# One run of up to 16 KB per partition instead of rows of 4 KB: the weight loads of a three-layer block on one Trainium2 core

## The chip, the cores and the metric

The kernel runs on one core of one Trainium2 chip. The metric is the time on the device of one execution, in microseconds; three runs of the kernel before are given. A profile is one more execution, recorded by the hardware profiler, with its own span. Rates are in GB/s of 10^9 bytes; a load of 2 MB means 2 x 1024 x 1024 bytes, which is 16 KB for each of the 128 partitions of the on-chip memory.

## What is computed

All in float32, on 256 tokens of 1024 features. First a block with attention in three branches (compressed, selected, window) beside a short convolution, and then a mixture of 64 experts, two of which serve each token:

```python
h = rms_norm(x, norm1_w) * (1 + sc1) + sh1
proj = h @ w_in
mix = rms_norm(concat(nsa_attention(...), short_conv(...)))
x = x + g1 * (mix @ w_out)
h2 = rms_norm(x, norm2_w) * (1 + sc2) + sh2
x = x + g2 * hier_moe(h2, ...)   # sum over a token's experts: weight * ((silu(h2 @ w1[e]) * (h2 @ w3[e])) @ w2[e])
```

Then two more layers: one mixes with a Fourier transform and a window attention that also sees 256 context tokens, the other with pooling; each is followed by a gated FFN of 2816 hidden features, `(silu(h @ w1) * (h @ w3)) @ w2`, and a last norm closes the whole. The shifts, scales and gates (`sh`, `sc`, `g`) of every layer are `silu(c) @ ada_w + ada_b`, 6 x 1024 columns a layer.

Of the weights the experts are the bulk: w1, w3 and w2 of 64 experts are 64 x 3 x 2 MB = 402.7 MB of the 589.5 MB that the DMA engines move.

## The kernel before

The host lays the inputs out (`_pack_inputs`) and the kernel computes. Nearly all weights pass through one ring of six buffers (`RING = 6`), the tiles named `w` of 128 partitions x 4096 floats, 16 KB a partition, 2 MB each. `wslot` takes the next buffer and issues one load from SyncE (SP), at L438 in the profile; the load waits until the engines have read what was in that buffer six loads ago. SP issues the loads in the order in which the program asks for them, on one queue that 16 DMA engines serve together. The program's order on the other engines is fixed at build time; a small model of the time (`_Model`, `weave`) orders the work of the front and of the second block, and its times for the loads are counted from the bytes of a slot.

The stages are, in order: the front (modulation, projections, attention, routing of the first block), the experts, the second block's Fourier and attention layer (`even`), its FFN, the pooling layer, and the last FFN. The expert stage runs over 16 quads of four experts. A quad gathers up to 32 tokens for each of its experts (tiles `xg`), multiplies them by w1 and w3 (`quad_h`, output `ps<-w,xg`), gates (`g`, `gT`), multiplies by w2 (`ps<-w,gT`), and adds the weighted results to `x`. `load_experts` brings each of the three weights of a quad in four loads; a load holds, for every partition, a part of the rows of all four experts, cut at L1435:

```python
src = self.a[n][4 * q:4 * q + 4].rearrange("e (p c k) f -> p c e (k f)", c=4, k=m)
```

So a partition of a slot is filled from four places in DRAM, one per expert, 2 MB apart, each a row of 4 KB. Twelve such loads make a quad. The first quad's third weight part that does not fit the ring (`EXTRA`) goes to four small tiles `piece`, and the last load of the stage is made as two halves of 1 MB with rows of 2 KB.

Before quad 8 stands a loop for experts with more than 32 tokens (`overflow`, its branch at L1523). It runs zero times on this input, but its branch is a meeting of all engines, and SP's part in it waits for the landing of all loads that SP has issued.

Other weights come as follows: the modulation weights (`w_ada`, `ada_w_2`, function `ada_rows`) in rows of 4 KB, four to a partition, their first two loads in rows of 2 KB; the projections (`win`, `wout`, `win2`, `wout2`) in rows of 4 KB per tile of 128 columns, the first in halves of 2 KB; the first weights of the compression (`cw1`) in rows of 1 KB; the second FFN weight (`f2`) in rows of 4 KB. The first FFN weight (`f13`) has already one run of 16 KB per partition.

Of the kernel before, what the change touches and what calls it, by code (L numbers as in the profile page):

```python
# [16 lines left out]
P = 128  # L17
# [27 lines left out]
# ------------------------------------------------------------------ layouts  # L45
# [158 lines left out]

def _pack_inputs(x):
# [6 lines left out]
    w = x["w_in"][0][:, _win_cols()].reshape(KT, P, 20, P)  # L212
    ins["win"] = np.ascontiguousarray(w.transpose(2, 1, 0, 3))
    ins["wval"] = x["w_in"][0][:, _val_cols()].reshape(KT, P, 280).transpose(1, 0, 2)
    w = x["w_out"][0][_mix_perm()].reshape(KT, P, KT, P)
    ins["wout"] = np.ascontiguousarray(w.transpose(2, 1, 0, 3))
    ins["w_ada"] = x["w_ada"][0]
# [6 lines left out]
    w = x["mix_in_w_2"][0][:, tiles].reshape(KT, P, 10, P)  # L224
    ins["win2"] = w.transpose(2, 1, 0, 3)
    rows = np.concatenate([np.arange(512), 512 + _mix_perm()[:512]])
    w = x["mix_out_w_2"][0][rows].reshape(KT, P, KT, P)
    ins["wout2"] = w.transpose(2, 1, 0, 3)
# [3 lines left out]
    ins["f2"] = x["ffn_w2_2"].reshape(2, NC, 2, P, D)  # L232
# [24 lines left out]
class _Model:  # L257
    """estimates when the engines are done with what has been issued so far"""
# [27 lines left out]
    def ready(self, *aps, engine="tensor", write=False):  # L286
        """when an engine can read (or write) them"""
# [8 lines left out]
    def last(self, name):  # L296
        """the last access of a tile so far"""
# [35 lines left out]
class _Net:  # L333
# [19 lines left out]
    # ---- small helpers  # L353
# [9 lines left out]
    def room(self, tag, n=1):  # L363
        """when the next n banks are free, for weave"""
# [5 lines left out]
    def grab(self, tag="g", n=1):  # L370
        """the next n banks, kept until release()"""
# [54 lines left out]
    def wslot(self, src, load=None):  # L426
        """next slot of the weight ring, filled from src ([128, ...] in DRAM)"""
        t = self.ring.tile([P, 4096], F32, tag="w", name=self.nm("w"))
        shape = src.shape
        n = int(np.prod(shape[1:]))  # L430
        dst = t[:, :n]
        if len(shape) == 3:
            dst = dst.rearrange("p (a b) -> p a b", a=shape[1])
        elif len(shape) == 4:
            dst = dst.rearrange("p (a b c) -> p a b c", a=shape[1], b=shape[2])
        self.slots_us.append(self.more_us + n * 512 / 360e3)
        self.more_us = 0.0
        d = self.nc.sync.dma_start(dst if load is None else dst[:, :, load], src if load is None else src[:, :, load])  # L438
        self.loads.append(d)
# [6 lines left out]
    def at(x, k):  # L446
        """feature tile k of x, a tile [128, 8, n] or a list of its feature tiles"""
# [28 lines left out]
    def loaded(self, n):  # L476
        """when slot n of the ring has arrived, for weave"""
# [12 lines left out]
    def front_slots(self, name, srcs, load=None):  # L490
        """slots of the ring ahead of their use: number and tile"""
        for src in srcs:
            self.ahead.setdefault(name, []).append((len(self.slots_us), self.wslot(src, load)))
# [12 lines left out]
    def event(self, name, *aps):  # L506
        """when an event has come and these are ready, for weave"""
        return lambda: self.ready(*aps) if name in self.events else math.inf

    # ---- setup  # L510
    def setup(self):
# [8 lines left out]
        # the scale of half the features, and the weight that meets them  # L520
        win0 = self.front_src("win0")
        for h in range(2):
            self.front_slots("ada1", [a["w_ada"][:, D + 512 * h:D + 512 * h + 512].rearrange("(k p) f -> p k f", p=P)])
            half = slice(512 * h, 512 * h + 512)
            if h == 0:
                self.front_slots("win0", [win0], load=half)
            else:
                nc.sync.dma_start(self.ahead["win0"][0][1][:, :, half], win0[:, :, half])
# [7 lines left out]
        # silu of the conditions  # L536
# [44 lines left out]
    def ada_cols(self, slots, h, st, bias, out):  # L581
        """512 columns of the same, in one slot"""
# [23 lines left out]
    def ada2(self, i):  # L606
        """part i of the modulation of layer 0, for the tokens and the context"""
# [3 lines left out]
    def gemv0(self, i):  # L611
        o = slice(8 * i, 8 * i + 8)
        yield from self.gemv(None, 0, self.sil[:, :8], self.vec("b_ada")[:, o], self.mod0[:, o], f"ada{i}")
        self.events[f"ada{i}"] = self.ready(self.mod0[:, o])

    def gemv(self, w, col0, c, bias=None, out=None, slots=None):
        """1024 columns of cond @ w + bias as a column tile [128, 8], on the vector engine; in steps.
        Without out, the sum over the partitions and the bias are left for later"""
        nc = self.nc
        acc = self.ph(D, "acc")  # L620
        for h in range(2):
            if slots:
                t = yield from self.take(slots, h)
            else:
                t = self.wslot(w[512 * h:512 * h + 512, col0:col0 + D].rearrange("(k p) f -> p k f", p=P))
# [31 lines left out]
    def gemv2(self, layer, i):  # L657
        o = 48 * layer + 8 * i
        return self.gemv(self.a["ada_w_2"][layer], D * i, self.sil[:, 8:16], self.vec("ada_b_2")[:, o:o + 8],
                         self.mod2[:, o:o + 8])  # L660
# [10 lines left out]
    def squares(self, x):  # L671
        """sum over the feature tiles of x * x"""
# [8 lines left out]
    def norm(self, x, acc=None):  # L681
        """1 / rms of the tokens of x [128, 8, 256] (feature major), on every partition; acc: its squares, summed"""
# [12 lines left out]
    def scaled(self, w, scale):  # L695
        """w * (1 + scale) per feature"""
# [4 lines left out]
    def norm_mod(self, x, s, shift, out=None, parts=None, acc=None):  # L701
        """x / rms * s + shift per feature, to out or as two float32r parts"""
# [27 lines left out]
    def bias_table(self):  # L730
        """T[p, h, j] = bias of head h at distance p + 128 - j"""
# [14 lines left out]
    def headnorm(self, src, w, outs, newton=False, tag="n"):  # L746
        """src [128, n] over the rms of its 64 row groups, times w; outs: (rows, tile) pairs"""
# [18 lines left out]
    def front_src(self, n):  # L766
# [3 lines left out]
        if n == "kv":  # L770
            return a["win2"][0:2].rearrange("t p k f -> p t (k f)")
        c = int(n[-1])
        if n[:-1] == "conv":
            return a["win"][8 + 3 * c:11 + 3 * c].rearrange("t p k f -> p t (k f)")
        if n[:-1] in ("win", "wout"):
            return a[n[:-1]][4 * c:4 * c + 4].rearrange("t p k f -> p t (k f)")
        return a["cw1"][c].rearrange("(j p) f -> p j f", p=P)

    def front_loads(self):
        a = self.a  # L780
        for n in ORDER:
# [5 lines left out]
            if n[:3] == "ada":  # L787
                w = a["ada_w_2"][0] if len(n) > 4 else a["w_ada"]
# [5 lines left out]
            self.front_slots(n, srcs)  # L794

    def proj(self):
        """the input projection of the tiles that run ahead of the shift of the modulation"""
# [5 lines left out]
        self.kz = self.ph(0, "kz", shape=[P, 2, S])  # rows (group, feature); branch, key  # L803
# [10 lines left out]
        self.wint = [self.ahead[f"win{c}"][0][1][:, i, :] for c in range(2) for i in range(4)]  # L814
# [10 lines left out]
        def tiles():  # L825
            for c in range(2):
# [3 lines left out]
                for k in range(KT):  # L830
# [4 lines left out]
                    for i in range(4):  # L835
                        self.mm(ps[i][:, :S], lhsT=self.wint[4 * c + i][:, P * k:P * k + P], rhs=h[:, k, :],
# [11 lines left out]
    def share(self):  # L848
        """the shift: its share in the tiles that ran ahead of it, and h; then the blocks to compress"""
# [6 lines left out]
        for c in range(2):  # L856
# [3 lines left out]
            for k in range(KT):  # L860
                j = k % 4
                self.mm(ps[32 * j:32 * j + 32, :], lhsT=sh[:, k, :], rhs=t0[:, :, P * k:P * k + P], start=k < 4, stop=k > 3,
                        tile_position=(0, 32 * j))
# [23 lines left out]
        # (v g0, v g1, k g0, k g1), half, block, pair  # L887
        A = self.A = self.ph(0, "A", shape=[P, 4, S]).rearrange("p c (i b j) -> p c i b j", i=2, j=8)
        for c in range(4):
# [5 lines left out]
            for i, rows in enumerate((LOW, HIGH)):  # L895
                # token 16 b + 2 j (+ 1 in the upper rows), j within the half
# [6 lines left out]
    def qk(self, i):  # L903
        """a tile of q (i < 4), k_slc or k_win"""
# [6 lines left out]
    def values(self):  # L911
        """v_slc, v_win and the gates: token major"""
# [17 lines left out]
    def hidden(self):  # L930
        """hidden layer of the compression"""
# [1096 lines left out]
```

## Time and profile before

| | us |
|---|---|
| median of 3 runs | 1760.09 (1758.51 to 1763.04) |
| span of the profiled execution | 1758.2 |
| of it: PE (matrix multiplies) busy | 1349.1 |
| VectorE (DVE) busy | 575.0 |
| ScalarE (ACT) busy | 375.8 |
| GpSimd (POOL) busy | 143.2 |
| data moved by DMA | 589.5 MB, mean 335 GB/s |

The page of a profile cuts the span into 40 slices of 44 us and gives for each the busy tenths of every engine, of the 16 DMA engines, and the GB/s moved. Its chain of waits follows the work that ended last back to what released it. A window is a stretch of the span in us from its start. The DMA view of a window counts packets, by sizes, and the bytes that began in it; a packet is one run of contiguous bytes to one partition on one DMA engine, and a few packets of 4 bytes are the signals that a load has landed. Time to landing is counted from the issue of a load to the arrival of its last byte, time in the queue included.

### The profile page before, as it was taken

What the parts mean: (1) busy time and instruction counts of PE and PEld (TensorE: products, weight loads), DVE (VectorE), ACT (ScalarE), POOL (GpSimd) and SP (SyncE); (2) the same over time, 40 slices, a digit from 0 to 9 for tenths busy, and PEclk for the clock granted to TensorE, in tenths of its full rate; (3) what the DMA queues carried; (4) which work ended last, traced back from release to release, by engine and by line L of the source; (5) the groups of instructions that cost most, each with busy time, mean ns of one, the idle gap of its engine ahead of it and who ended that gap; (6) DMA issues with size and microseconds to landing.
All of it is one profiled execution on the core that took longest, in us unless ns stands there. A gap on an engine that the chain in (4) does not pass through costs nothing.

```text
span 1758.2 us, 18422 instructions
## 1 busy us (share of the span) xinstructions
PE 1349.1 (77%) x7664; PEld 782.4 (45%) x7664; DVE 575.0 (33%) x1109; ACT 375.8 (21%) x704; POOL 143.2 (8%) x80
## 2 busy tenths in 40 slices
PE   7999976665675665566667566658998999999997
PEld 5676832221221221221122122215676787778886
DVE  1567711110110111011011011103766787554443
ACT  2345210000000000100000000003324444544444
POOL 0000000000000000000000000000201323212224
PEclk9999988888887888688888788889998999999999
DMA  9787999999999999899999999999476787635610
GB/s 380 252 335 300 343 361 408 409 409 409 409 409 409 409 409 409 323 409 409 409 409 408 409 409 409 409 409 388 166 266 251 276 335 300 260 144 191 264 72 24
DMA packets 144811, 589.51 MB, mean 335 GB/s; under 512 B 4840, under 2 KB 9064, under 8 KB 141136
## 3 DMA queue, kind: packets, MB, share of 16 engines
q1 hardware_dynamic: 143584, 584.82, 84.7%
q0 software_dynamic: 704, 2.64, 0.4%
q8 instruction: 63, 1.03, 0.2%
q10 hardware_dynamic: 432, 0.79, 0.1%
q14 instruction: 28, 0.23, 0.0%
HBM read 587.16 MB, written 1.06 MB: 335 GB/s over the span
## 4 chain that ended last, share of the span: by engine, by line
PE 33%; DMA 22%; DVE 3%; ACT 1%; issue 0%; DVEq 0%; ACTq 0%
PE ps L250 33%; DMA w<-in_w 21%; DVE acc L250 1%; DMA w<-in_ada_w 0%; DVE wlo L250 0%; DVE p L250 0%; ACT p L250 0%; DVE x L250 0%; ACT rstd L250 0%; DVE ada L250 0%; DVE sqa L250 0%; DVE mix L250 0%; ACT mix L250 0%; ACT sq L250 0%; DVE nt L250 0%
## 5 line engine op out<-in xcount | busy, mean ns | idle before, releaser
L250 PE MATMUL ps<-w,xg 128*32 128x512 f32 x2032 | 303.5, 734 | 210.1 <-DMA w<-in_w 210.1
L250 PE MATMUL ps<-w,gT 128*32 128x512 f32 x1024 | 177.6, 830 | 120.1 <-DMA w<-in_w 113.5
L250 PEld LDWEIGHTS ps<-w,xg 128*32 128x32 f32 x2032 | 65.2, 125 | 430.9 <-DMA w<-in_w 218.9
L250 ACT ACTIVATE whi<-w 128x1024 fp32r<-128x1024 f32 x132 | 139.4, 1059 | 151.4 <-PE ps L250 145.8
L250 DVE TENSOR_TENSOR g<-g,ps 128x512 f32<-128x512 f32 x16 | 11.0, 688 | 482.5 <-PE ps L250 482.5
L250 DVE TENSOR_TENSOR wlo<-w,whi 128x1024 fp32r<-128x1024 f32 x88 | 114.7, 1311 | 111.5 <-ACT whi L250 111.4
L250 PEld LDWEIGHTS ps<-w,gT 128*32 128x32 f32 x1024 | 33.7, 136 | 247.4 <-DMA w<-in_w 163.5
L250 PE MATMUL ps<-whi,mix 128*128 128x512 f32 x352 | 140.0, 403 | 4.1 <-ACT mix L250 4.1
L250 DVE SCALAR_TENSOR_TENSOR acc<-w,sil,acc 128x1024 f32<-128x1024 f32 x98 | 141.8, 1447 | 2.3 <-DMA w<-in_ada_w 0.8
L250 POOL TENSOR_TENSOR wlo<-w,whi 128x1024 fp32r<-128x1024 f32 x44 | 112.8, 2573 | 349.2 <-ACT whi L250 292.2
L250 PE MATMUL ps<-wlo,mix 128*128 128x512 f32 x352 | 140.4, 400 | 0.0
L250 PE MATMUL ps<-whi,xl 128*128 128x512 f32 x352 | 138.4, 398 | 0.5 <-DVE xl L250 0.5
L250 DVE COPY y<-ps 128x512 f32<-128x512 f32 x16 | 11.1, 692 | 294.6 <-PE ps L250 294.6
L250 PE MATMUL ps<-hT,w 128*128 128x256 f32 x320 | 79.1, 395 | 2.4 <-DVE hT L250 2.4
L250 ACT ACTIVATE gT<-ps 128x512 f32<-128x512 f32 x16 | 9.6, 597 | 329.3 <-PE ps L250 329.3
L250 PEld LDWEIGHTS ps<-whi,mix 128*128 128x128 f32 x352 | 67.3, 191 | 22.2 <-ACT mix L250 5.3
L250 DVE SCALAR_TENSOR_TENSOR x<-ps,mod,x 128x256 f32<-128x256 f32 x152 | 67.0, 482 | 28.0 <-PE ps L250 28.0
L250 PEld LDWEIGHTS ps<-whi,xl 128*128 128x128 f32 x352 | 67.3, 191 | 16.1 <-DVE xl L250 1.2
L250 PE MATMUL ps<-oh,xtok 128*128 128x128 f32 x512 | 62.0, 281 | 15.9 <-DVE oh L250 15.9
L250 PEld LDWEIGHTS ps<-wlo,mix 128*128 128x128 f32 x352 | 67.4, 191 | 14.6 <-DVE wlo L250 0.4
L250 PE MATMUL ps<-wlo,gh 128*128 128x512 f32 x176 | 69.7, 399 | 0.0
L250 PE MATMUL ps<-whi,gl 128*128 128x512 f32 x176 | 69.1, 397 | 0.0
(302 smaller groups left out, 1489.3 us busy)
## 6 DMA issues: line engine op xcount, KB each, us to landing
w<-in_w SPq DMA_DIRECT2D x190, 2048.0 KB, 23.9
w<-in_f SPq DMA_DIRECT2D x32, 2048.0 KB, 8.4
w<-in_ada_w SPq DMA_DIRECT2D x24, 2048.0 KB, 10.3
w<-in_w_ada SPq DMA_DIRECT2D x12, 2048.0 KB, 11.3
w<-in_wout SPq DMA_DIRECT2D x4, 2048.0 KB, 8.6
w<-in_win SPq DMA_DIRECT2D x3, 2048.0 KB, 19.0
w<-in_win SPq DMA_DIRECT2D x4, 1536.0 KB, 11.9
w<-in_win SPq DMA_DIRECT2D x4, 1024.0 KB, 14.6
```

Source lines behind the costliest of these rows:

```text
L250: r = f(*args, **kw)
```

## The change

The host lays every weight out in DRAM in the order in which a slot holds it, so that the source of a load is one run per partition. An expert load becomes `src[c]` of an array of shape [16 quads, 4 parts, 128 partitions, 4096 floats]: 16 KB in one run, a slot of 2 MB contiguous in DRAM. The modulation weights, the projections, the compression weights and the second FFN weight are treated in the same way; slots that are not full have runs of 8 or 12 KB. The first projection's two halves and the last expert load's two halves become runs of 8 KB, and their views in the kernel (`wint`, the `rhs` of w2) read the new places. `EXTRA`'s pieces and the loop's pieces keep runs of 4 KB and 2 KB. Comments and docstrings are taken out as well.

The core of the diff:

```diff
-    ins["cw1"] = np.stack([x["cmp_v_w1"][0], x["cmp_k_w1"][0]])
+    w = np.stack([x["cmp_v_w1"][0], x["cmp_k_w1"][0]])
+    ins["cw1"] = w.reshape(2, 16, P, 256).transpose(0, 2, 1, 3)
     for n in ("w1", "w3"):
-        ins[n] = x[n][0].reshape(E, KT, P, FE).transpose(0, 2, 1, 3).reshape(E, D, FE)
-    ins["w2"] = x["w2"][0]
-    ins["ada_w_2"] = x["ada_w_2"]
+        ins[n] = x[n][0].reshape(NQUAD, 4, 4, 2, P, FE).transpose(0, 2, 4, 1, 3, 5).reshape(NQUAD, 4, P, 4 * D)
+    w = x["w2"][0].reshape(NQUAD, 4, P, 4, D).transpose(0, 3, 2, 1, 4).reshape(NQUAD, 4, P, 4 * D)
+    last = w[-1, -1].reshape(P, 4, 2, 512).transpose(2, 0, 1, 3).reshape(2, P, 2 * D)
+    ins["w2"], ins["w2last"] = w, last
...
+    for n, w in (("ada0", x["w_ada"][0]), ("ada20", x["ada_w_2"][0]), ("ada21", x["ada_w_2"][1])):
+        ins[n] = w.reshape(2, 4, P, 6, D).transpose(3, 0, 2, 1, 4).reshape(6, 2, P, 4 * D)
...
     def load_experts(self, n, q):
         k = 4 if n == "w2" else 8
         m = k // 4
-        src = self.a[n][4 * q:4 * q + 4].rearrange("e (p c k) f -> p c e (k f)", c=4, k=m)
+        src = self.a[n][q]
...
-                last = (n, q, c) == ("w2", NQUAD - 1, 3)
-                w = self.wslot(src[:, c], slice(0, 512) if last else None)
-                if last:
-                    self.loads.append(self.nc.sync.dma_start(w[:, :, 512:], src[:, c, :, 512:]))
-                w = w.rearrange("p e (k f) -> p e k f", k=m)
+                w = self.wslot(src[c]).rearrange("p (e k f) -> p e k f", e=4, k=m)
...
     @staticmethod
     def ada_rows(w, i, h):
-        return w[512 * h:512 * h + 512, D * i:D * i + D].rearrange("(k p) f -> p k f", p=P)
+        return w[i, h].rearrange("p (k f) -> p k f", k=4)
...
-            w2 = self.wslot(self.a["f2"][layer, c:c + n].rearrange("c j p d -> p (c j) d"))
+            src = self.a["f2"][layer, c // 2] if c < NC - 1 else self.a["f2last"][layer]
+            w2 = self.wslot(src).rearrange("p (j d) -> p j d", d=D)
```

PE, DVE, ACT and POOL have the same instructions in the same order with the same waits. On SP, too, the loads stand in the same order with the same waits; only their shapes differ. Here is SP's row of loads in the expert stage up to the loop's branch, first before (w2 of quad 7, w1 of quad 8, the load of the loop count, the branch):

```order
L438 DMA w607_3122<-in_w2 128x4x1024
L438 DMA w608_3124<-in_w2 128x4x1024
L438 DMA w609_3126<-in_w2 128x4x1024
L438 DMA w626_3265<-in_w1 128x4x1024
L438 DMA w627_3267<-in_w1 128x4x1024
L438 DMA w628_3269<-in_w1 128x4x1024
L438 DMA w629_3271<-in_w1 128x4x1024
L1522 TENSOR_LOAD extra_3281
L1523 COMPARE_AND_BRANCH
```

The same place on SP now:

```order
L453 DMA w607_3122<-in_w2 128x4096
L453 DMA w608_3124<-in_w2 128x4096
L453 DMA w609_3126<-in_w2 128x4096
L453 DMA w626_3265<-in_w1 128x4096
L453 DMA w627_3267<-in_w1 128x4096
L453 DMA w628_3269<-in_w1 128x4096
L453 DMA w629_3271<-in_w1 128x4096
L1545 TENSOR_LOAD extra_3281
L1546 COMPARE_AND_BRANCH
```

Nothing moved: each load has one row of 4096 floats where it had four of 1024.

## Rows read from the trace of the kernel before

**Rows 1.** The page's 40 slices: busy tenths of PE and DMA, then GB/s.
```profile
PE   7999976665675665566667566658998999999997
...
DMA  9787999999999999899999999999476787635610
GB/s 380 252 335 300 343 361 408 409 409 409 409 409 409 409 409 409 323 409 409 409 409 408 409 409 409 409 409 388 166 266 251 276 335 300 260 144 191 264 72 24
```

**Rows 2.** The page's chain that ended last: share by engine, then the line by line.
```profile
PE 33%; DMA 22%; DVE 3%; ACT 1%; issue 0%; DVEq 0%; ACTq 0%
PE ps L250 33%; DMA w<-in_w 21%; DVE acc L250 1%; DMA w<-in_ada_w 0%; DVE wlo L250 0%; DVE p L250 0%; ACT p L250 0%; DVE x L250 0%; ACT rstd L250 0%; DVE ada L250 0%; DVE sqa L250 0%; DVE mix L250 0%; ACT mix L250 0%; ACT sq L250 0%; DVE nt L250 0%
```

**Rows 3.** The chain in order of time: start us, us, what.
```profile
888.10 12.76 PE ps L250 x83
...
900.86 23.04 DMA w<-in_w
```

**Rows 4.** Waits, whole span: who for whom, us in total, times, longest.
```profile
PEld ps L250 <- DMA w<-in_w: 382.4, 108, 5.6
...
PE ps L250 <- DMA w<-in_w: 323.6, 142, 4.7
```

**Rows 5.** Windows of the expert stage: length, busy us of each engine, PEclk, DMA share, GB/s.
```profile
225.00:714.00 489.00, 303.25 (x1971) 106.23 (x1970) 57.09 (x136) 27.81 (x58) 0.00 (x0) 0.84 1.02 407
719.00:1191.00 472.00, 300.99 (x1912) 102.26 (x1911) 52.34 (x123) 28.36 (x57) 0.00 (x0) 0.84 1.02 407
```

**Rows 6.** DMA packets in 6:14, 49:60, 300:700, 1502:1504, 1504:1512, 1505:1511 us, in turn.
```profile
DMA packets 1591, 3.15 MB, mean 394 GB/s; under 512 B 56, under 2 KB 56, under 8 KB 1590
...
DMA packets 3731, 3.83 MB, mean 349 GB/s; under 512 B 17, under 2 KB 3728, under 8 KB 3728
...
DMA packets 41158, 163.62 MB, mean 409 GB/s; under 512 B 1251, under 2 KB 1251, under 8 KB 41144
...
DMA packets 24, 0.39 MB, mean 197 GB/s; under 512 B 0, under 2 KB 0, under 8 KB 0
...
DMA packets 220, 3.34 MB, mean 418 GB/s; under 512 B 16, under 2 KB 16, under 8 KB 16
...
DMA packets 172, 2.56 MB, mean 426 GB/s; under 512 B 16, under 2 KB 16, under 8 KB 16
```

**Rows 7.** DMA, whole span: a queue's packets, MB, share; issues, KB each, us to landing.
```profile
q8 instruction: 63, 1.03, 0.2%
...
w<-in_w SPq DMA_DIRECT2D x190, 2048.0 KB, 23.9
w<-in_f SPq DMA_DIRECT2D x32, 2048.0 KB, 8.4
...
piece<-in_w SPq DMA_DIRECT2D x4, 512.0 KB, 5.6
w<-in_w SPq DMA_DIRECT2D x2, 1024.0 KB, 20.1
```

**Rows 8.** SP's queue in order of time: start us, us, issues and their number.
```profile
186.45 25.89 SPq L438 DMA_DIRECT2D w<-in_w  x5
212.44 12.08 SPq L1442 DMA_DIRECT2D piece<-in_w  x4
224.76 74.92 SPq L438 DMA_DIRECT2D w<-in_w  x17
```

**Rows 9.** DVE around the loop's branch, in order of time; in brackets idle before, releaser.
```profile
701.76 0.15 DVE L250 CAST extra<-rc 128x1 int32<-128x1 f32 x1
716.40 0.76 DVE L250 TENSOR_TENSOR oh<-R,slots 128x256 f32<-128x256 f32 x2 [14.48 <-SPq L1523]
```

**Rows 10.** Windows in the front and of the first FFN, columns as in Rows 5.
```profile
50.00:100.00 50.00, 47.97 (x341) 33.76 (x341) 30.79 (x95) 20.85 (x57) 1.85 (x3) 1.00 0.71 251
...
1312.00:1531.00 219.00, 212.01 (x974) 167.15 (x973) 160.08 (x172) 100.49 (x136) 59.26 (x22) 0.98 0.75 288
```

**Rows 11.** DVE at the start of the first FFN, in order of time.
```profile
1329.89 1.28 DVE L250 SCALAR_TENSOR_TENSOR acc<-w,sil,acc 128x1024 f32<-128x1024 f32 x1 [0.60 <-DMA w<-in_ada_w]
```

More of the change, by code (lines that the diff above doesn't have):

```diff
@@ L202, in _vectors, with _tiles4 @@
     return v
+def _tiles4(w):
+    w = w.reshape(KT, P, 2, 4, P)
+    return w.transpose(2, 1, 3, 0, 4).reshape(2, P, 4 * D)
 def _pack_inputs(x):
@@ L211, in _pack_inputs @@
     ins["ctxT"] = np.ascontiguousarray(x["ctx_2"][0].T.reshape(KT, P, S).transpose(1, 0, 2))
-    w = x["w_in"][0][:, _win_cols()].reshape(KT, P, 20, P)
-    ins["win"] = np.ascontiguousarray(w.transpose(2, 1, 0, 3))
+    w = x["w_in"][0][:, _win_cols()].reshape(KT, P, 20, P).transpose(1, 2, 0, 3)
+    ins["win0"] = w[:, :4].reshape(P, 4, 2, 4, P).transpose(2, 0, 1, 3, 4).reshape(2, P, 4 * 512)
+    ins["win1"] = w[:, 4:8].reshape(P, 4 * D)
+    ins["conv"] = w[:, 8:].reshape(P, 4, 3 * D).transpose(1, 0, 2)
@@ L226, in _pack_inputs @@
+    ins["kv"] = w[:, :2].reshape(P, 2 * D)
+    ins["win2"] = w[:, 2:].reshape(P, 2, 4 * D).transpose(1, 0, 2)
     rows = np.concatenate([np.arange(512), 512 + _mix_perm()[:512]])
-    w = x["mix_out_w_2"][0][rows].reshape(KT, P, KT, P)
-    ins["wout2"] = w.transpose(2, 1, 0, 3)
+    ins["wout2"] = _tiles4(x["mix_out_w_2"][0][rows])
     ins["pool_w"] = x["pool_w_2"][0].reshape(4, 2, P, 256).transpose(2, 0, 1, 3)
@@ L424, in vec, with wslot @@
         return self.vect[:, o:o + w]
[L426 to L435, printed above, removed]
+    def wslot(self, *srcs):
+        t = self.ring_tile = self.ring.tile([P, 4096], F32, tag="w", name=self.nm("w"))
+        n = 0
+        for i, src in enumerate(srcs):
+            shape = src.shape
+            m = int(np.prod(shape[1:]))
+            dst = t[:, n:n + m]
+            if len(shape) == 3:
+                dst = dst.rearrange("p (a b) -> p a b", a=shape[1])
+            elif len(shape) == 4:
+                dst = dst.rearrange("p (a b c) -> p a b c", a=shape[1], b=shape[2])
+            n += m
+            d = self.nc.sync.dma_start(dst, src)
+            self.loads.append(d)
         self.slots_us.append(self.more_us + n * 512 / 360e3)
         self.more_us = 0.0
-        d = self.nc.sync.dma_start(dst if load is None else dst[:, :, load], src if load is None else src[:, :, load])
-        self.loads.append(d)
+        if len(srcs) > 1:
+            dst = t[:, :n]
         if self.hold is not None:
@@ L488, in loaded, with front_slots @@
         return when
-    def front_slots(self, name, srcs, load=None):
+    def front_slots(self, name, srcs, view=None):
         for src in srcs:
-            self.ahead.setdefault(name, []).append((len(self.slots_us), self.wslot(src, load)))
+            n, t = len(self.slots_us), self.wslot(src)
+            self.ahead.setdefault(name, []).append((n, t if view is None else t.rearrange("p (a b) -> p a b", a=view)))
     def take(self, name, h=0):
@@ L519, in setup @@
         self.more_us += 2.9
-        win0 = self.front_src("win0")
         for h in range(2):
-            self.front_slots("ada1", [a["w_ada"][:, D + 512 * h:D + 512 * h + 512].rearrange("(k p) f -> p k f", p=P)])
-            half = slice(512 * h, 512 * h + 512)
+            self.front_slots("ada1", [a["ada1h"][h]])
             if h == 0:
-                self.front_slots("win0", [win0], load=half)
-            else:
-                nc.sync.dma_start(self.ahead["win0"][0][1][:, :, half], win0[:, :, half])
+                self.front_slots("win0", [a["win0"][0]])
+                w = self.ring_tile
+                self.slots_us[-1] *= 2
+            else:
+                nc.sync.dma_start(w[:, 2048:], a["win0"][1])
+        n, _ = self.ahead["win0"][0]
+        self.ahead["win0"][0] = n, w.rearrange("p (h t f) -> p t h f", h=2, t=4)
         self.cont = self.keep.tile([P, a["con"].shape[1]], F32, name="cont")
@@ L612, in gemv0, with gemv @@
         o = slice(8 * i, 8 * i + 8)
-        yield from self.gemv(None, 0, self.sil[:, :8], self.vec("b_ada")[:, o], self.mod0[:, o], f"ada{i}")
+        yield from self.gemv(None, self.sil[:, :8], self.vec("b_ada")[:, o], self.mod0[:, o], f"ada{i}")
         self.events[f"ada{i}"] = self.ready(self.mod0[:, o])
-    def gemv(self, w, col0, c, bias=None, out=None, slots=None):
+    def gemv(self, w, c, bias=None, out=None, slots=None):
         nc = self.nc
@@ L624, in gemv @@
             else:
[L625 removed]
+                t = self.wslot(w[h]).rearrange("p (k f) -> p k f", k=4)
             for kk in range(4):
@@ L658, in gemv2 @@
         o = 48 * layer + 8 * i
-        return self.gemv(self.a["ada_w_2"][layer], D * i, self.sil[:, 8:16], self.vec("ada_b_2")[:, o:o + 8],
+        return self.gemv(self.a[f"ada2{layer}"][i], self.sil[:, 8:16], self.vec("ada_b_2")[:, o:o + 8],
                          self.mod2[:, o:o + 8])
@@ L769, in front_src @@
             return a["wval"]
[L770 to L777, printed above, removed]
+        if n in ("kv", "win1"):
+            return a[n]
+        return a["cw1" if n[:-1] == "cw" else n[:-1]][int(n[-1])]
     def front_loads(self):
@@ L813, in proj @@
         self.front_loads()
-        self.wint = [self.ahead[f"win{c}"][0][1][:, i, :] for c in range(2) for i in range(4)]
+        w0 = self.ahead["win0"][0][1]
+        self.wint = [[w0[:, i, k // 4, P * (k % 4):P * (k % 4) + P] for k in range(KT)] for i in range(4)]
+        w1 = self.ahead["win1"][0][1]
+        self.wint += [[w1[:, i, P * k:P * k + P] for k in range(KT)] for i in range(4)]
         sc = self.wk(KT, "mods")
@@ L861, in share @@
                 j = k % 4
-                self.mm(ps[32 * j:32 * j + 32, :], lhsT=sh[:, k, :], rhs=t0[:, :, P * k:P * k + P], start=k < 4, stop=k > 3,
-                        tile_position=(0, 32 * j))
+                w = t0[:, :, P * k:P * k + P] if c else t0[:, :, k // 4, P * (k % 4):P * (k % 4) + P]
+                self.mm(ps[32 * j:32 * j + 32, :], lhsT=sh[:, k, :], rhs=w, start=k < 4, stop=k > 3, tile_position=(0, 32 * j))
             self.done(f"win{c}")
@@ L1441, in load_experts @@
                 for e in range(4):
-                    self.nc.sync.dma_start(t[-1][e], src[:, c, e].rearrange("p (k f) -> p k f", k=m))
-            else:
-                last = (n, q, c) == ("w2", NQUAD - 1, 3)
-                w = self.wslot(src[:, c], slice(0, 512) if last else None)
-                if last:
-                    self.loads.append(self.nc.sync.dma_start(w[:, :, 512:], src[:, c, :, 512:]))
-                w = w.rearrange("p e (k f) -> p e k f", k=m)
+                    self.nc.sync.dma_start(t[-1][e].rearrange("p k f -> p (k f)"), src[c, :, D * e:D * e + D])
+            elif (n, q, c) == ("w2", NQUAD - 1, 3):
+                w = self.wslot(*[self.a["w2last"][h] for h in range(2)])
+                w = w.rearrange("p (h e f) -> p e h f", h=2, e=4)
+                t.append([w[:, e:e + 1] for e in range(4)])
+            else:
+                w = self.wslot(src[c]).rearrange("p (e k f) -> p e k f", e=4, k=m)
                 t.append([w[:, e] for e in range(4)])
-        return lambda j, k: t[k // m][j][:, k % m, :]
+        return lambda j, k: t[k // m][j][:, k % m]
     def piece_experts(self, n, q):
@@ L1492, in quad @@
                 for j in range(4):
-                    self.mm(py[n][32 * j:32 * j + 32, :], lhsT=gT[:, f, 32 * j:32 * j + 32],
-                            rhs=wt[j][:, 512 * n:512 * n + 512], start=f == 0, stop=f == 3, tile_position=(0, 32 * j))
+                    rhs = wt[j][:, n] if len(wt[j].shape) == 3 else wt[j][:, 512 * n:512 * n + 512]
+                    self.mm(py[n][32 * j:32 * j + 32, :], lhsT=gT[:, f, 32 * j:32 * j + 32], rhs=rhs, start=f == 0, stop=f == 3,
+                            tile_position=(0, 32 * j))
         nc.scalar.activation(y[:, :512], py[0], AF.Copy)
@@ L1740, in gemvs2 @@
             o = 8 * i
-            yield from self.gemv(None, 0, self.sil[:, 8:16], self.vec("ada_b_2")[:, o:o + 8], self.mod2[:, o:o + 8], f"ada2_{i}")
+            yield from self.gemv(None, self.sil[:, 8:16], self.vec("ada_b_2")[:, o:o + 8], self.mod2[:, o:o + 8], f"ada2_{i}")
             self.events[f"ada2_{i}"] = True
@@ L1796, in even @@
             if i == 3:
-                self.front_slots("out2", [a["wout2"][4 * c:4 * c + 4].rearrange("t p k f -> p t (k f)") for c in range(2)])
-            self.front_slots(f"ada2_{i}", [self.ada_rows(a["ada_w_2"][0], i, n) for n in range(2)])
+                self.front_slots("out2", [a["wout2"][c] for c in range(2)], 4)
+            self.front_slots(f"ada2_{i}", [self.ada_rows(a["ada20"], i, n) for n in range(2)])
         self.mix = self.wk(0, "mix", 1, shape=[P, KT, S])
@@ L2008, in run @@
         self.pool_mixer()
-        self.ffn(1, self.gemv(a["ada_w_2"][1], 5 * D, self.sil[:, 8:16]), 6, out)
+        self.ffn(1, self.gemv(a["ada21"][5], self.sil[:, 8:16]), 6, out)
         self.stack.close()
```

32 lines of the change are left out of this document (16 added, 16 removed).

## The prediction

> **What bounds the kernel now.** I read the page's forty slices first. In 20 of the 21 slices from the seventh on the DMA engines stand at 9 tenths and move 408 to 409 GB/s (one has a dent, 323 GB/s), while PE is busy 5 to 7 tenths; before and after that PE is at 7 to 9 tenths and the rate wanders below 400 [rows 1]. The chain that ended last agrees: 22% of the span is DMA, nearly all of it loads into the ring from w1, w3 and w2, and the rest of what matters is PE [rows 2]. In order of time the chain in the expert stage alternates between stretches of PE, 12.76 us and less, and waits of some 23 us for a load [rows 3], and PE with its weight load stands idle 323.6 and 382.4 us behind those loads (the two overlap) [rows 4].
>
> The windows fix the stage. From 225 to 714 us and from 719 to 1191 us the 16 DMA engines are full (share 1.02) at 407 GB/s, and PE is busy 303 and 301 us of 489 and 472 [rows 5]. In the middle of the first, from 300 to 700 us, the page counts 41158 packets and 409 GB/s: the runs of 4 KB [rows 6]. The median load of 2 MB lands 23.9 us after its issue [rows 7], though it needs only 2097152 B / 409 GB/s = 5.13 us by itself: some 4.7 loads stand queued. So the queue never runs dry, and in this stage the time is bytes over rate. PE could take more: (303 + 301) / 16 = 37.8 us for a quad of experts, against 12 x 5.13 = 61.5 us for its loads.
>
> **What the change does to the expert stage.** It takes nothing away but the cuts: the same bytes, in the same order, with the same waits; PE, VectorE, ScalarE and GpSimd have the same instructions in the same order. The one thing to price is a packet of 16 KB in place of four of 4 KB. The kernel before has stretches with other runs. One load after another of 1 KB runs (the compression weights, from 49 to 60 us) moves 349 GB/s, of 2 KB runs (from 6 to 14 us) 394, of 4 KB runs 409, and the first FFN weight, which has runs of 16 KB already, 426 from 1505 to 1511 us, when a second such load stands queued behind the first [rows 6]. The longer the run, the faster, at every step.
>
> As time of a packet on one of 16 engines: 16 x 1024 / 349 = 46.9 ns, 16 x 4096 / 409 = 160.2 ns. The difference, 113.3 ns for 3 KB, is 37.8 ns per KB, which leaves 9.2 ns that each packet costs whatever its length. At 16 KB that gives 16 x 37.8 + 9.2 = 613 ns, or 427 GB/s, an estimate from these rows that meets the direct 426. I take 427, since a direct reading over 6 us is only good to about a packet and the two agree. A load of 2 MB then takes 4.91 us instead of 5.13, 0.215 us less.
>
> How many loads: 190 of 2 MB, two halves of 1 MB and four pieces of 0.5 MB make 192 ring loads' worth [rows 7]. Five and the four pieces (6 in worth) go out before 224.76 us [rows 8], when PE is the bound, so 186 remain; 186 x 5.13 = 954 us, which is the two stretches (961 us) less their ramps. The gain is **186 x 0.215 = 40.0 us**. Bounds: with the packet's fixed cost gone wholly 37.8 ns per KB is left, 4.83 us a load, and the gain is 54.7 us; with the 2 KB and 4 KB rows alone (83.2 and 160.2 ns) the fixed cost is 6.1 ns, a 16 KB packet takes 623 ns, 421 GB/s, and the gain is 27 us. The window a little wider than the best, 1504 to 1512 us, shows 418 [rows 6], with the start of the burst in it, 20.6 us; a full ring has no such start, so I keep it for a rival.
>
> The Trainium skill, "DMA: Bandwidth & Descriptors", section "Why small descriptors are slow (HBM only)", speaks for less: about 3 cycles for a packet on a bus that moves 32 B each cycle, worth caring for at 256 B or below. By it a 16 KB run takes 515 cycles where four of 4 KB take 524, 1.7%, an estimate of 16 us here. The trace doesn't agree: the rule puts 1 KB runs 7% behind 4 KB runs, and the rows say 17% (349 against 409).
>
> **The break at 714 us.** Before quad 8 all engines meet at the branch of the overflow loop, and SP passes it only when every load issued so far has landed; the next transfer starts after it, and DVE resumes at 716.40 after 14.48 us [rows 9]. The engines' last result before the meeting, a conversion on DVE at 701.76, is 14 us older, so it is the landings that set it. They come sooner by their share of the 40 us and the break moves with them; I cost it at nothing.
>
> **Outside the expert stage.** In the front the compression weights go from 1 KB to 16 KB runs (4 MB, 12.0 to 9.8 us), the first modulation weights from 2 KB to 16 KB (4 MB, 1 us less) and others from 4 KB to 8, 12 or 16 KB. The list of waits names no load of the ring in that part, and PE is busy 47.97 of 50 us from 50 to 100 [rows 10]: I count nothing; without PE's work as a cover it would be a gain of 3 us. In the first FFN PE is busy 212 of 219 us [rows 10]. One wait for a modulation weight stands on the chain: DVE waits 0.60 us at 1329.89 [rows 11]; a landing sooner by three loads' 0.2 us gives it back, 0.5 us. The last expert load comes in two halves with 2 KB runs, now 8 KB: at 394 GB/s it took 5.32 us, with 8 x 37.8 + 9.2 = 312 ns a packet 4.98, 0.1 us beyond what is counted. The instruction queue q8 shares the engines (63 packets, 1.03 MB) [rows 7]; each could stand behind one packet of 0.61 instead of 0.16 us, 28 us if every one were waited for singly. No row shows an engine waiting for one, so I take 0.
>
> Sum: 40.0 + 0.5 + 0.1 = 40.6. The profiled span of 1758.2 us becomes 1717.6; the median of the runs is 1.9 us above that span, so the forecast is **1719.5 us**.
>
> **The rivals.** *Half of it*: 16 KB packets hold only the 418 GB/s of the wider window, because each seam between loads costs something. 1760.1 - 20.6 = 1739.5. For it: the dip at the start of a burst; against: 426 over a stretch that has a seam in it [rows 6].
>
> *No change*: 409 GB/s is the ceiling of the memory or of the path into the core, and not of the packets; 1759.5. Against: 426 in the same trace, short as it is. The same page, section "Specifications", gives 512 B as the least transfer for line rate, by which 4 KB runs would have nothing to gain; the 1 KB row, at 349, is against it.
>
> *Slower*: a load of 16 KB runs starts badly. From 1502 to 1504 us, its first 2 us, the rate is 197 GB/s [rows 6], and the FFN loads, two thirds of them with such runs, land a median 8.4 us after issue where 2 MB should take 4.9 [rows 7]. The loss is 2 x (426 - 197) / 426 = 1.07 us for a load that starts so. From 0.2 / 1.07 = one load in five the gain is gone; with every second load it is 186 x (0.54 - 0.205) = 62 us slower, 1822. Place: the first packets on each DMA engine at a seam in the ring's queue. Against: the queue is 4.7 loads deep in the expert stage, and in the FFNs, where the loads start so, it is empty.
>
> That PE becomes the bound has no chance of its own: 12 x 4.91 = 58.9 us for a quad is still far above 37.8, which was at a mean granted clock of 0.84 [rows 5].
>
> **How the numbers follow.** Forecast with its bounds (27 to 51 us of gain, 1709 to 1733): 0.80. More than that: 0.04, as the fixed cost of a packet can't fall below zero (1705). Half: 0.07. No change: 0.04. Slower: 0.05. The range is 1708 to 1734. What this kernel's measurement can tell from no change is about 0.3%, 5 us; so faster 0.91, same 0.04, slower 0.05.
>
> **What would show it.** In the profile after, the slices of the expert stage stand at 425 to 429 GB/s instead of 409, with a third or fewer of the 144811 packets; its two stretches last some 469 and 451 us; a load of the experts lands in 22 to 23 us, still queued; PE's idle time behind those loads falls by about 40 us; the front up to 225 us and the 567 us behind 1191 keep their lengths within 2 us. It is wrong if the rate rises and the stretches don't shorten (then PE or the ring binds somewhere inside a quad), or if the rate stays at 409, or if dips return every 5 us at the seams.

## The result, and the profile after

The changed kernel takes 1719.16 us (median of 4 runs, 1716.67 to 1721.72) where the kernel before, run beside it, takes 1759.3 us: 0.9769 of its time, 95% interval 0.9758 to 0.9781. The forecast was 1719.5. The profiled execution has a span of 1719.5 us (1758.2 before).

First the page's slices of the kernel after: busy tenths of PE and of the DMA engines, GB/s, packets, and the chain's shares by engine. They answer to [rows 1, 2].

```profile
PE   7999976666765765666576676769989999999997
...
DMA  9687889999999999899999999997476786635620
GB/s 402 244 342 300 317 370 427 427 426 426 427 428 427 427 426 425 340 427 426 426 426 427 428 427 427 426 426 285 184 298 243 301 340 260 245 147 220 245 74 25
DMA packets 43563, 589.51 MB, mean 343 GB/s; under 512 B 4840, under 2 KB 4968, under 8 KB 6992
...
PE 31%; DMA 24%; DVE 3%; ACT 1%; issue 0%; DVEq 0%; ACTq 0%
```

The same bytes move in 43563 packets instead of 144811. The slices of the expert stage stand at 425 to 428 GB/s where they stood at 408 to 409, with the one dent of the loop's break (340), and the DMA engines are as full as before: the stage is still bound by them, at a higher rate. DMA's share of the chain went up all the same, from 22% to 24%: the chain counts a load from its issue to its landing, and that grew (below).

The windows of the two stretches and of what follows (length, busy us of PE, PEld, DVE, ACT, POOL, granted clock, DMA share, GB/s), to be held against [rows 5]:

```profile
225.00:693.00 468.00, 309.83 (x1970) 107.98 (x1968) 57.55 (x136) 27.64 (x57) 0.00 (x0) 0.82 1.00 425
699.00:1151.00 452.00, 305.80 (x1910) 104.93 (x1909) 52.72 (x123) 28.33 (x57) 0.00 (x0) 0.81 1.00 425
1151.00:1719.50 568.50, 534.68 (x2532) 420.66 (x2532) 335.37 (x457) 240.83 (x379) 137.81 (x66) 0.97 0.57 224
```

The first stretch holds the same 1970 or so matrix multiplies in 468 us instead of 489, the second in 452 instead of 472. In the two together PE is busy 615.6 us instead of 604.2, at a granted clock of 0.82 and 0.81 instead of 0.84. The edges of these windows are set by eye. The stage itself begins with the first multiply by w1, at 228.89 us before and 228.42 after, and ends with the last one by w2, here before and after:

```profile
1198.29 1.06 PE L250 MATMUL ps<-w,gT 128*32 128x512 f32 x8
```
```profile
1157.21 1.07 PE L264 MATMUL ps<-w,gT 128*32 128x512 f32 x8
```

So the stage takes 929.9 us instead of 970.5, 40.6 us less, and what follows it 561.3 us instead of 558.8. DVE around the loop's branch, against [rows 9]:

```profile
680.84 0.15 DVE L264 CAST extra<-rc 128x1 int32<-128x1 f32 x1
695.96 0.76 DVE L264 TENSOR_TENSOR oh<-R,slots 128x256 f32<-128x256 f32 x2 [14.97 <-SPq L1546]
```

DVE resumes behind the branch at 695.96 us instead of 716.40, 20.44 us sooner, and waited 14.97 instead of 14.48 us: the break moved almost whole.

Last, the waits for loads [rows 4] and the landings [rows 7]:

```profile
PEld ps L264 <- DMA w<-in_w: 355.4, 107, 5.4
PE ps L264 <- DMA w<-in_w: 269.2, 131, 4.5
...
DVE acc L264 <- DMA w<-in_ada: 1.4, 2, 1.1
```

```profile
w<-in_w SPq DMA_DIRECT2D x190, 2048.0 KB, 26.1
```

PE's wait fell from 323.6 to 269.2 us, its weight load's from 382.4 to 355.4. PE's fell by 54 us, more than the 40 forecast, as PE was busy 11 us longer in a stage that is 41 us shorter. The time from issue to landing, though, went **up**, from 23.9 to 26.1 us, with loads that are shorter. That was not forecast; it comes back below.

### The profile page after: what moved, and what is told of

The parts are those of the page before. It is cut to its first block, busy times and chain, and to the rows that moved or that the text cites. A ratio compares the mean times of both kernels' runs of the same rounds, so it can differ in the third digit from the quotient of the medians.

```text
span 1719.5 us, 18422 instructions
## 1 busy us (share of the span) xinstructions
PE 1361.6 (79%) x7664; PEld 788.7 (46%) x7664; DVE 575.8 (33%) x1109; ACT 375.6 (22%) x704; POOL 143.0 (8%) x80
## 2 busy tenths in 40 slices
DMA packets 43563, 589.51 MB, mean 343 GB/s; under 512 B 4840, under 2 KB 4968, under 8 KB 6992
## 4 chain that ended last, share of the span: by engine, by line
PE 31%; DMA 24%; DVE 3%; ACT 1%; issue 0%; DVEq 0%; ACTq 0%
PE ps L264 31%; DMA w<-in_w 22%; DMA w<-in_w2last 1%; DVE acc L264 1%; DMA w<-in_ada 0%; DVE wlo L264 0%; DVE p L264 0%; ACT p L264 0%; DVE x L264 0%; ACT rstd L264 0%; DVE ada L264 0%; DVE sqa L264 0%; DVE mix L264 0%; ACT mix L264 0%; ACT sq L264 0%
## 5 line engine op out<-in xcount | busy, mean ns | idle before, releaser
L264 PEld LDWEIGHTS ps<-wlo,mix 128*128 128x128 f32 x352 | 67.6, 192 | 14.6 <-DVE wlo L264 0.4
L264 PEld LDWEIGHTS ps<-oh,xtok 128*128 128x128 f32 x512 | 61.8, 200 | 18.1 <-DVE oh L264 16.5
## 6 DMA issues: line engine op xcount, KB each, us to landing
w<-in_w SPq DMA_DIRECT2D x190, 2048.0 KB, 26.1
```

The costliest lines, as they stand in the source:

```text
L264: r = f(*args, **kw)
```

## Experiments

Base of all but the first is the changed kernel. The arrays, slots and matrix multiplies are the same unless the text says otherwise. A rate given for a run is that from 300 to 640 us of its trace, inside the expert stage.

**The expert loads alone.** The kernel before, with only the layout of w1, w3 and w2 changed.

```diff
-        src = self.a[n][4 * q:4 * q + 4].rearrange("e (p c k) f -> p c e (k f)", c=4, k=m)
+        src = self.a[n][q]
```

> The kernel before, with the new layout for w1, w3 and w2 alone (one run of 16 KB per partition of an expert load); all other weights, and the two halves of the last expert load (2 KB runs), as before. Theory: the whole gain is the expert loads, 186 of them at 4.91 instead of 5.13 us, so 1759.3 - 40 = 1719 us, and within 3 us of the changed kernel. Rival: the other loads (front, second block, FFNs) give part of the gain; then this stays above 1725.

Measured: 1721.05 us, 0.9782 of the kernel before (0.9765 to 0.9798), 427 GB/s. The whole gain is there, with the front, the second block and the FFNs still on their old rows.

**All but the expert loads.** The complement: expert weights in the old layout, everything else new.

```diff
-        src = self.a[n][q]
+        src = self.a[n][4 * q:4 * q + 4].rearrange("e (p c k) f -> p c e (k f)", c=4, k=m)
```

> The changed kernel with the old layout for w1, w3 and w2 alone (rows of 4 KB from four places in DRAM, the last load's halves with 2 KB runs): the complement of the run with the experts alone. Theory: 1759 us, within 3 us of the kernel before, with 409 GB/s in the expert stage. Rival: the other loads matter; then it is below 1754, or, if 16 KB runs elsewhere cost something, above 1764.

Measured: 1760.69 us, 1.0002 of before (0.9992 to 1.0012), 409 GB/s. So the longer runs in the front, where the rate rose from 380 to 402 GB/s in the first slice, and in the FFNs are worth nothing that can be measured. That PE is the bound there rests on its busy time [rows 10].

**Two, four and eight runs per partition.** A load stays one piece of 2 MB in DRAM, cut into 2, 4 or 8 blocks of 128 shorter runs; `RUNS` is 2, 4, 8. This parts the length of a packet from the nearness of addresses.

```diff
+    for n in ("w1", "w3", "w2"):
+        ins[n] = ins[n].reshape(NQUAD, 4, P, RUNS, 4 * D // RUNS).transpose(0, 1, 3, 2, 4)
...
+    def part(self, n, q, c, lo, hi):
...
+        src, m = self.a[n][q, c], 4 * D // RUNS
...
+        return src[lo // m:hi // m].rearrange("r p f -> p r f")
...
-                w = self.wslot(src[c]).rearrange("p (e k f) -> p e k f", e=4, k=m)
+                self.wslot(self.part(n, q, c, 0, 4 * D))
+                w = self.ring_tile.rearrange("p (e k f) -> p e k f", e=4, k=m)
```

> The changed kernel with expert loads of two runs of 8 KB per partition; a load is still 2 MB in one piece of DRAM (its first half holds the first runs of all partitions, its second half the second). Theory of a fixed cost of 9.2 ns per packet: 37.8 x 8 + 9.2 = 312 ns a packet, 421 GB/s, 4.99 us a load, 186 x 0.075 = 14 us more than the changed kernel, 1733 us. Rival, that the gain comes from the load being one piece of DRAM and not from the length of the runs: 1719 us.

> The same with four runs of 4 KB per partition: the packets of the kernel before, but a load is one piece of 2 MB in DRAM instead of four places 2 MB apart. Theory of the packets: 409 GB/s and 1759 us, the kernel before. Rival (contiguous DRAM is what counts): 427 GB/s and 1719 us. A time between would divide the gain between the two.

> The changed kernel with expert loads of eight runs of 2 KB per partition, a load still one piece of 2 MB in DRAM. Theory of a fixed cost per packet: 37.8 x 2 + 9.2 = 84.8 ns, 386 GB/s, 5.43 us a load, 186 x 0.52 = 97 us more than the changed kernel, 1816 us; by the 394 GB/s that such runs showed in the front of the kernel before, 5.32 us and 1796 us. Rival (contiguous DRAM counts): 1719 us. A second thing is asked: in the kernel before the expert loads were issued 23.9 us before they landed, in the changed one 26.1 us, though a load is shorter now. If SP can put only so many packets into the queue (23.9 / 5.13 = 4.7 loads of 512 packets, some 2400), then with 1024 packets a load the issue comes only 2.3 loads, some 12.6 us, before the landing; if the ring's buffers are the limit, it stays at 24 us or more.

The DMA view of 300 to 640 us, in the order after (16 KB), 8 KB, 4 KB, 2 KB; of each kernel one row:

```profile
DMA packets 9962, 145.12 MB, mean 427 GB/s; under 512 B 1104, under 2 KB 1104, under 8 KB 1104
```
```profile
DMA packets 18508, 142.82 MB, mean 420 GB/s; under 512 B 1086, under 2 KB 1086, under 8 KB 1086
```
```profile
DMA packets 34988, 139.08 MB, mean 409 GB/s; under 512 B 1066, under 2 KB 1066, under 8 KB 34976
```
```profile
DMA packets 65093, 131.41 MB, mean 386 GB/s; under 512 B 1006, under 2 KB 1006, under 8 KB 65081
```

| run, KB | GB/s expected | GB/s | us expected | us measured | ratio to before |
|---|---|---|---|---|---|
| 16 | 427 | 427 | 1719.5 | 1719.16 | 0.9769 (0.9758 to 0.9781) |
| 8 | 421 | 420 | 1733 | 1735.0 | 0.986 (0.9843 to 0.9876) |
| 4 | 409 | 409 | 1759 | 1758.37 | 0.9994 (0.9984 to 1.0003) |
| 2 | 386 | 386 | 1816 | 1817.0 | 1.0332 (1.0302 to 1.0362) |

With 4 KB runs the gain is gone, though the load is one contiguous piece. It was the number of packets: the DMA engines are full in all four windows (share 1.01, 1.01, 1.02 and 1.04). One line, 37.8 ns per KB and 9.2 ns per packet, drawn through the 1 KB and 4 KB windows of the kernel before, gives all four rates to 1 GB/s.

**The same runs, 1 MB apart.**

```diff
+    for n in ("w1", "w3", "w2"):
+        ins[n] = ins[n].transpose(2, 0, 1, 3)
...
-        src = self.a[n][q]
+        src = self.a[n].rearrange("p q c f -> q c p f")[q]
```

> The changed kernel with the same runs of 16 KB, but in DRAM the 64 loads of a weight lie side by side in each partition's row: the 128 runs of a load are 1 MB apart instead of next to each other. Theory of the packets: the distance doesn't count, 427 GB/s and 1719 us. [...]

Measured: 1723.29 us (two runs, 1721.82 and 1724.77), 0.9799 (0.9771 to 0.9828), 427 GB/s. The rate is that of neighbouring runs, and the interval of the time overlaps that of the changed kernel. From 225 to 300 us the rate is 414 GB/s instead of 423, and the stage takes 932.5 us in this trace instead of 929.9; what makes these 2.6 us stays open. The Trainium skill, "DMA: Bandwidth & Descriptors", section "Latency and other measured facts", has copies between tensors in DRAM that slow down as the pitch of the rows grows: 207 GB/s at 512 KiB, 164 at 2 MiB, 103 at 4 and 8 MiB. Such copies and pitches of 2 MiB and more weren't tried here.

**Five buffers instead of six.**

```diff
-        self.ring = pool("ring", RING)
+        self.ring = pool("ring", RING - 1)
```

> The changed kernel with five buffers in the ring instead of six. Theory: the queue still holds 26.1 - 4.9 = some 21 us of loads at every issue, so the expert stage keeps 427 GB/s and its length; only the front, where PE waits for nothing in the ring now, may lose a few us: 1719 to 1725 us. Rival, that part of the gain is the deeper queue (26.1 against 23.9 us from issue to landing) and not the shorter packets: the stage's rate falls below 427 and the time goes up by 10 us or more.

Measured: 1737.92 us (two runs, 1735.14 and 1740.70), 0.9883 (0.9842 to 0.9924), 13 us above the upper end of what was expected. The windows 50 to 100, 225 to 300 and 300 to 640 us of this run, columns as above:

```profile
50.00:100.00 50.00, 39.88 (x290) 26.80 (x288) 25.16 (x75) 19.60 (x51) 1.85 (x3) 0.97 0.55 213
...
225.00:300.00 75.00, 54.96 (x407) 28.00 (x409) 18.43 (x72) 10.43 (x23) 0.00 (x0) 0.92 0.94 387
300.00:640.00 340.00, 224.06 (x1389) 74.83 (x1382) 39.55 (x91) 18.29 (x38) 0.00 (x0) 0.82 1.01 427
```

The last two of the changed kernel, with six buffers:

```profile
225.00:300.00 75.00, 53.47 (x394) 20.07 (x396) 9.68 (x24) 6.68 (x13) 0.00 (x0) 0.88 1.01 423
300.00:640.00 340.00, 230.95 (x1432) 80.36 (x1436) 42.39 (x98) 19.77 (x42) 0.00 (x0) 0.81 1.01 427
```

In the middle of the expert stage the theory held: 427 GB/s, with the loads landing 21.2 us after their issue. Most of the loss lies before the stage, and it is one wait. SP issues two loads of modulation weights at 60.72 and 87.76 us with six buffers, and only at 87.00 and 87.43 us with five; DVE stands until the first has landed. SP's rows with six and with five buffers, then DVE's with five:

```profile
60.72 27.37 SPq L453 DMA_DIRECT2D w<-in_ada  x2
```
```profile
87.00 0.96 SPq L453 DMA_DIRECT2D w<-in_ada  x2
...
96.58 0.75 DVE L264 TENSOR_SCALAR acc<-w,sil 128x1024 f32<-128x1024 f32 x1 [12.13 <-DMA w<-in_ada]
```

From 50 to 100 us PE is busy 39.88 us, where it was 47.97 with six buffers, and the first expert multiply starts at 240.38 us instead of 228.42, 12.0 us late. SP's queue shows the expert pieces going out at 225.48 us

```profile
225.48 11.96 SPq L1463 DMA_DIRECT2D piece<-in_w  x4
```

where the changed kernel has them at 211.94; the first quads then start with less in the ring (387 GB/s from 225 to 300 us, 423 with six). The stage loses another 9.4 us in this trace, 6.7 of them before DVE resumes behind the break (714.64 us) and 2.7 after it. So the sixth buffer is worth most in the front, and in the stage not through the rate of a full queue. My guess that the front had only a few us to lose was wrong.

**Half of every expert load.** Experts 2 and 3 of a quad use the weights of 0 and 1, so half of the bytes of a load are left out and the output is another; all multiplies stay.

```diff
-                w = self.wslot(src[c]).rearrange("p (e k f) -> p e k f", e=4, k=m)
-                t.append([w[:, e] for e in range(4)])
+                w = self.wslot(src[c, :, :2 * D]).rearrange("p (e k f) -> p e k f", e=2, k=m)
+                t.append([w[:, e % 2] for e in range(4)])
```

> The changed kernel with only half of every expert load (8 KB per partition, the last load of all whole): experts 2 and 3 of a quad use the weights of experts 0 and 1, so the output is another. All matrix multiplies stay. It asks how far the stage could go before PE is the bound. A quad's loads take 12 x 2.5 = 30 us; PE was busy 37.8 us a quad at a mean clock of 0.84. Theory: PE and its dependences become the bound at 38 to 44 us a quad instead of 58.9, 16 x (58.9 - 41) = 290 us less, some 1430 us, and PE's idle time behind loads nearly vanishes. Rival: something else in the quad (the gather, the gate, the write back) holds it above 50 us a quad, 1580 us or more; then the changed kernel was close to another bound.

Measured: 1298.35 us (one run), 421 us less than the changed kernel and 130 less than expected. The window 300 to 640 us of this run, and PE's and PEld's waits for loads, whole span:

```profile
300.00:640.00 340.00, 310.31 (x2573) 136.51 (x2565) 73.79 (x175) 36.75 (x74) 0.95 (x1) 0.97 0.96 389
...
PEld ps L264 <- DMA w<-in_w: 13.6, 20, 1.6
PE ps L264 <- DMA w<-in_w: 1.9, 5, 0.7
```

The waits for loads are nearly gone, and PE is busy 310 of 340 us. It handles 2573 multiplies there; the same window of the changed kernel (shown above) has 1432 in 230.95 us of busy time. So one takes 0.121 us of PE instead of 0.161. The mean granted clock is 0.97 instead of 0.81, and that alone would make 0.161 x 0.81 / 0.97 = 0.134; taken over PE's busy time only, the clock is 0.98 instead of 0.77, which makes 0.126. A quad has some 243 multiplies (3883 in the 16 quads of [rows 5]) and takes 340 x 243 / 2573 = 32 us. My figure of 38 to 44 us was taken at the clock of a PE that waits. Nothing else in a quad holds the stage above 32 us. How far below that PE alone could go this run doesn't say: its DMA engines are busy too (share 0.96), and 12 loads of 1 MB need 30 us at the 420 GB/s of 8 KB runs.

## Why the prediction was right, point by point

**What bounds the stage: right.** Bytes over rate, in both stretches. The runs with 8, 4 and 2 KB follow 186 loads times the time of a load to 2 us, from 1719 to 1817 us; the one with runs 1 MB apart is 4 us above. One reading was loose: the pieces of some 23 us in the chain [rows 3] are not waits but loads from issue to landing, and PE and its weight load waited 5.6 us for a load at the longest [rows 4].

**The price of a packet: right, and the size too.** 0.215 us a load was the step; the stage's rate came out at 427, as taken. The stretches, forecast as 469 and 451 us, are 468 and 452, and the stage as a whole is 40.6 us shorter. That the whole kernel hit to less than 1 us (40.6 us forecast, 40.1 measured) is luck, as runs of one kernel spread over 5 us. The bounds on both sides (27 and 54.7 us) were wider than needed: the pair of 2 KB and 4 KB windows, which gave 6.1 ns a packet and the lower bound, was the poor one. The 2 KB run in the expert stage moves 386 GB/s, and not the 394 of the window in the front: 2 MB at 386 take 5.43 us, 84.8 ns a packet, 9.2 ns of it fixed. A window of 8 us at the start of the program was 2% off the rate of a long queue.

**The rule of the Trainium skill: too small here.** Three cycles a packet ("DMA: Bandwidth & Descriptors", section "Why small descriptors are slow (HBM only)") would have given 16 us, an estimate. With the 32 bytes of metadata that the section adds for each operation, taken as one cycle more, it would be an estimate of 22 us. The runs give 40 us, and their four rates 9.2 ns a packet. By the Trainium skill's 512 B for line rate (same page, section "Specifications"), as the prediction reads it, 4 KB and 16 KB runs should not differ; they do, 409 against 427 GB/s. The rival that 409 was the ceiling of something else fell with the first full slice of the stage, at 427.

**The break: right.** It moved with the landings, 20.44 us at its end; the rest of the stage gained as much again (20.7 us).

**Outside the stage: right that nothing is gained, wrong in the 0.5 us.** All but the expert loads together give 1.0002. The one wait on the chain that was to vanish, 0.60 us [rows 11], grew. Here is the same instruction with the new layout for the experts alone, and then in the changed kernel:

```profile
1290.43 1.29 DVE L250 SCALAR_TENSOR_TENSOR acc<-w,sil,acc 128x1024 f32<-128x1024 f32 x1 [0.59 <-DMA w<-in_ada_w]
```
```profile
1290.85 1.28 DVE L264 SCALAR_TENSOR_TENSOR acc<-w,sil,acc 128x1024 f32<-128x1024 f32 x1 [1.09 <-DMA w<-in_ada]
```

With the old layout outside the experts the wait is 0.60 and 0.59 us, in the two traces that have it; in seven with the new one it is 0.96 to 1.52 us (with five buffers DVE waits at another instruction). So the step that failed in this term is that longer runs would bring this landing sooner; why they don't stays open.

The time behind the last expert multiply is longer by 2.5 us, a little beyond the 2 us forecast. Over the ten traces of this case it goes from 558.7 to 561.5 us, in no order of the layouts: 558.8 before, 561.0 with the experts alone, 558.7 with runs 1 MB apart. Part of it shows in PE's rows. The kernel before, then the kernel after, the same multiplies in the Fourier and attention layer:

```profile
1270.02 1.09 PE L250 MATMUL ps<-p2T,vall 128*64 128x128 f32 x16
```
```profile
1229.55 1.98 PE L264 MATMUL ps<-p2T,vall 128*64 128x128 f32 x16
```

Sixteen records of multiplies take 1.98 us instead of 1.09, with no wait between. The windows of these places, before and after, in the columns used above:

```profile
1270.00:1273.00 3.00, 3.00 (x27) 2.33 (x26) 2.19 (x4) 0.00 (x0) 0.85 (x1) 1.00 0.08 10
```
```profile
1229.00:1233.00 4.00, 4.00 (x25) 2.97 (x24) 2.19 (x3) 0.00 (x0) 0.76 (x1) 0.67 0.34 74
```

The mean granted clock is 0.67 there and was 1.00: PE ran a part of these 4 us at the lower of its two levels, 1.2 GHz instead of 2.4. The same sixteen multiplies are slow, 1.35 to 1.98 us, in eight of the ten traces, with the old expert layout (first row) as well; with runs 1 MB apart (second row) they are not:

```profile
1270.23 1.98 PE L262 MATMUL ps<-p2T,vall 128*64 128x128 f32 x16
```
```profile
1232.03 1.09 PE L266 MATMUL ps<-p2T,vall 128*64 128x128 f32 x16
```

So I don't put the dip down to the length of the expert loads' runs. Whether the kernel before has it in other executions no trace shows.

**The rivals.** The slow start at seams did not occur in a full queue: no slice of the stage dips but the one with the break, and 427 GB/s is what the packets alone cost, which leaves nothing for the seams. That a stretch with a seam in it had shown 426 was the right row to trust. Nor did q8's packets, priced at up to 28 us, cost anything that shows: the stage gained all that the loads' price gives. PE did not become the bound: a quad's loads still take 58.9 us, and with half the bytes a quad is done in 32.

**The landing: wrong.** I had 22 to 23 us, from the same depth of queue with shorter loads; it is 26.1. The step that failed is the depth: 26.1 / 4.91 = 5.3 loads stand queued, where it was 4.7. The view of SP's issues in 300 to 600 us (instructions, duration of one in ns: least, median, most), of the kernels before, after, with 8 KB and with 2 KB runs:

```profile
L438 SPq DMA_DIRECT2D w<-in_w x59: 453/4868/10251, 299.8 to 597.9; - x59
```
```profile
L453 SPq DMA_DIRECT2D w<-in_w x61: 327/328/328, 303.5 to 599.4; - x61
```
```profile
L456 SPq DMA_DIRECT2D w<-in_w x60: 367/368/497, 300.1 to 595.6; - x60
```
```profile
L456 SPq DMA_DIRECT2D w<-in_w x56: 3687/5245/7654, 296.8 to 598.1; - x56
```

With rows of 4 KB SP hung in the issue of a load for 4.87 us in the median, about the time of one load; with one run of 16 KB it is through in 0.33 us. Issues filled some 283 of the 300 us before the change, and 20 after. So before it SP was still busy with one load when it could have issued the next. After it the ring sets the depth: with five buffers the loads land 21.2 us after their issue, one load's time less than with six. That SP waits for room in a queue is my reading of the first; no run tested it. The late issue cost nothing that shows, as the queue stayed long enough: the rates of 8 and 16 KB runs, whose issues take 0.37 and 0.33 us, lie on one line with those of 2 and 4 KB, and between 8 and 16 KB the stage still differs by 15 us (944.7 and 929.9).

## What to carry to other kernels

Where the DMA engines are full, count packets: here each cost 9 ns on its engine, from 2 to 16 KB, so runs of 16 KB move 427 GB/s where 4 KB move 409 and 2 KB 386. Laying weights out on the host so that a buffer's partition is one run adds no work on the chip, and pays only in the stretch that is bound by bytes; the same edit elsewhere was worth nothing (1.0002, 0.9992 to 1.0012). Two windows of one trace with different run lengths gave the price before any run, but take them where the queue has been full for a while.

## What the runs showed that I had not expected

- The issue of a load on SP takes as long as a whole load when its runs are short: 4.87 us at 4 KB runs, 5.25 us at 2 KB, 0.37 and 0.33 us at 8 and 16 KB. What the limit counts stays open. I expected some 2400 packets, from 4.7 loads of 512 before; the 2 KB run landed its loads 19.8 us after issue, 3.6 loads of 1024, which fits neither that (12.6 us) nor a limit by the ring's buffers alone (24 us or more). The time to landing holds the issue itself; without it 19.0 us are left with 4 KB runs, 3.7 loads, and 14.6 us with 2 KB, 2.7 loads, which is no fixed number of packets either.
- Distance in DRAM did not matter to the rate in mid-stage for runs of 16 KB: 427 GB/s with the 128 runs of a load side by side or 1 MB apart.
- A wait for a load was longer where that load and those around it had longer runs: DVE's for a modulation weight in the first FFN is 0.60 and 0.59 us with the old layout there, and 0.96 to 1.52 us with the new one.
- One buffer of the ring is worth 12 us in a front that shows no wait for the ring: without it one load went out 26 us later.
- PE's granted clock is 0.81 in the expert stage, where it waits for loads, and 0.97 when half of the bytes are left out and it hardly waits. The time of a stage's multiplies under a transfer bound overstates what they take without it, here 37.8 against 243 x 0.121 = 29 us a quad.
